# w_down of an encoder layer: fewer pairs in the seven-product form, two pairs in direct form ahead of the tail, other queues and times for some loads and stores

## The chip, the cores and the metric

The kernel runs on one core of a Trainium2 chip. The metric is device time in microseconds (us) of one execution, as the median of several runs. Every profile is one execution under the hardware profiler; its times count from the first instruction's start.

A core has TensorE (matmuls; PE in the profile, PEld its weight loads), VectorE (DVE), ScalarE (ACT), GpSimd (POOL) and SyncE (SP). Each works through its own instructions in order. A transfer is issued by an engine's queue; here nearly all loads are on SP's queue, and those that add to memory on GpSimd's. A queue whose next transfer must wait for something holds up all that stand behind it.

## What is computed

One layer of an encoder on 512 tokens of width 2048, in fp32: a norm, mixed attention, a residual; then a norm, SwiGLU with hidden width 5632, a residual, and a last norm:

```python
    h = rmsnorm(x, ffn_norm_w[l])
    x = x + (jax.nn.silu(h @ w_gate[l]) * (h @ w_up[l])) @ w_down[l]
return rmsnorm(x, final_norm_w)
```

The change concerns the product with w_down (5632 x 2048) and what lies around it. Call g the product of the gated and the up branch; it is 5632 x 512, transposed.

## The kernel before

Every fp32 operand is split into a high part in the rounded type fp32r and a low part (the rest), and each product is three matmuls: high by high, high by low, low by high. ScalarE makes the high part (L196, L1101, L1328: a copy), VectorE the low part by a subtraction (L197, L1106, L1329).

**Gate and up.** `Feed.run` takes w_gate and w_up through 22 blocks of 256 columns. Its matmuls are L1147 to L1149. Two blocks of 256 by 256 by 256 are multiplied with seven products instead of eight; sums of the weights (L1089 to L1091) and of the operands are needed for it. `Feed.finish` multiplies gate and up (L1184, L1188) and writes the result to DRAM, gd[j] for pair j of 128 rows, with a store on SP's queue (L1190).

**w_down, three forms in a row.** The 5632 rows are 22 pairs of 256.

1. *Direct jobs*, `run_job` (L293 to L295): pairs 0 and 1, for each of four columns c of 512 outputs. A job is four halves (128 rows each); a half is 12 matmuls of 512 columns, 3 for each of four token tiles. `st.split(j.first + i + AHEAD)` with AHEAD = 3 splits the weights two halves ahead of the one in work. `g_load` (L1223) and `g_split` (L1231 to L1235) bring g. `evac_down` scales the four banks with ScalarE (L1262), and GpSimd adds them to xd in DRAM (L1264). Between the halves `before_down` calls `dn.make(3)`.
2. *Seven-product form*, class `Down` (L1362 to L1364): pairs 2 to 19 in three chunks of six; in a chunk the four columns, in a column the chunk's six pairs. One pair for one column is a *piece*, 42 matmuls of 256 columns into seven banks. Weights come by L1073 on SP, at most three ahead. `operands`, a generator, loads a pair of g (L1307) and makes its sums and splits (L1313 to L1329); each `make` takes it on to its next `yield`, four to a pair, and `Down.run` calls make(2) each piece. At a column's end ScalarE copies the seven banks out (L1379, L1381), three of them behind the next piece's split (`evac_late`). The first chunk stores them to md in DRAM by SP (L1386), the others add to md by GpSimd (L1384). In the last chunk `combine(c)` follows: seven loads of md (L1401, SP) and four of xd (L1404, GpSimd), two yields later VectorE's sums (L1410, L1411) and scaling (L1424) into x1[c]. It is stepped once a piece by `run_urgent`. The fourth combine, `self.done`, is not on that list; the tail runs it.
3. *Tail*, `finish` (L1515 to L1517): pairs 20 and 21 direct, token tile by token tile. Its weights are loaded by `st.load` (L181) and split by L196 and L197 from piece 2 of the last chunk's last column on, where also g is loaded and split, and the last norm's weights are loaded (`start_tail`). VectorE adds each bank to x1 (`residual`, L1254), ScalarE squares (L394), VectorE multiplies by the last norm's weights (L1524), and `later` scales by the norm's factor (L1501, L1499) and stores (L1502).

**What sets the order.** The code is written out in the order in which each engine has its instructions; there is no scheduler. SBUF is handed out in two pools of slots, 70 of 512 columns (a in the profile) and 16 of 1024 (b), first freed, first used: a transfer waits until the slot's last reader is done.

Of the kernel before, what the change touches and what calls it, by code (L numbers as in the profile page):

```python
# [111 lines left out]
def put(*slots):  # L112
    for s in slots:
        if s.home is not None:
            s.home.free.append(s.i)


def layer(nc, tc, x, attn_norm_w, w_in, rel_table, gw_f, gb_f, gw_b, gb_b, gla_norm_w, w_out,
# [7 lines left out]
    with tc.manual_schedule(), \  # L126
# [136 lines left out]
        def run_job(j):  # L263
# [6 lines left out]
            for i in range(j.n):  # L270
                if j.before:
                    j.before(i)
                st.load()
                st.split(j.first + i + AHEAD)
                _, _, wh, wl = st.halves[j.first + i]
# [836 lines left out]
        class Feed(Blocks):  # L1112
# [66 lines left out]
            def finish(self, u, c_, c):  # L1179
                w, j = self.units[u]  # L1180
                if w is w_gate:
                    tables(SILU)
                    for f in range(2):
                        dve.tensor_tensor(c_.t[:, f], c_.t[:, f], rb[2 + f].t, op=OP.mult)  # L1184
                    act.activation(c_.t, c_.t, AF.Silu)
                    self.gate = c_
                else:
                    dve.tensor_tensor(c_.t, c_.t, self.gate.t, op=OP.mult)  # L1188
                    put(self.gate)
                    sp.dma_start(out=gd[j], in_=c)  # L1190
                    put(c_)
# [47 lines left out]
        def down_start(q):  # L1239
            if q == 0:  # L1240
                g_load(0)
            if q == 1:
                st.until = down_pieces
                st.limit = 3
                st.load()
                g_load(1)
            if q == 2:
                g_split(0)
                st.split(down_first + 2)
            if q == 3:  # L1250
                dn.make(2)

# [33 lines left out]
        class Down(Blocks):  # L1286
# [13 lines left out]
            def operands(self):  # L1300
                a, z = slice(0, 256), slice(256, 512)
                tt = dve.tensor_tensor
                for q in [q for ch in self.chunks for q in ch]:
                    while len(s4.free) < 2:
                        yield
                    r = s4.get(F32, [P, 2, 512])
                    sp.dma_start(out=r.t.rearrange("p f t -> p (f t)"), in_=gd[q])  # L1307
                    yield
                    while len(s2.free) < 9 + 4:
                        yield  # L1310
                    n1, f2 = r.t[:, 1], r.t[:, 0]
# [11 lines left out]
                    for i, (src, hi, lo, hf) in enumerate(todo):  # L1323
# [6 lines left out]
                        if i:  # L1330
                            put((r, t13, t24)[i - 1])
                        if i % 2:
                            yield
# [55 lines left out]
            def evac_late(self):  # L1389
                for e in self.late:  # L1390
                    self.evac(*e)
                if self.late and self.late[0][0] == len(self.chunks) - 1:
                    self.done = self.combine(self.late[0][1])
                    if self.late[0][1] < 3:
                        urgent.append(self.done)
                self.late = []

            def combine(self, c):
# [4 lines left out]
                for t in range(4):  # L1403
                    pool.dma_start(out=x1[c][t].t, in_=xd[4 * c + t])  # L1404
                yield
                yield
                M = [None] + [x_.t for x_ in m]
# [22 lines left out]
            def run(self):  # L1430
                for i, (ch, c, q) in enumerate(self.seq):
# [12 lines left out]
                    if ch == len(self.chunks) - 1 and c == 3:  # L1444
                        n = self.chunks[ch].index(q)
                        if n == 0:
                            g_load(FF // 256 - 2)
                        if n == 1:
                            g_split(FF // 256 - 2)
                            g_load(FF // 256 - 1)  # L1450
                            st.until, st.limit = None, 1
                            start_tail()
                        if n == 2:
                            g_split(FF // 256 - 1)
                        if n >= 2:
                            st.load()
                            st.split(tail_first + 2 * (n - 1))
                self.evac_late()
                st.limit, st.big = 3, tail_first
                drain()  # L1460

# [4 lines left out]
        for c in range(4):  # L1466
            j = job("B", [piece512(w_down, c * 512, k) for k in (0, 2)], list(range(4)),
                    lambda k: gT[k], evac_down(c), before=before_down(c))
            if c == 3:
                j.drop = drop_g  # L1470
        down_pieces = len(st.pieces)
        tail_first = len(st.halves)
        dn = Down([list(range(2, 8)), list(range(8, 14)), list(range(14, 20))])

# [10 lines left out]
        def finish():  # L1485
# [6 lines left out]
            def later(t, ys):  # L1492
# [3 lines left out]
                for c in range(4):  # L1496
                    o = ys[c]
                    if t == 3 and c % 2:
                        act.activation(o.t, o.t, AF.Copy, scale=rstdf[:, t:t + 1])  # L1499
# [5 lines left out]
            def run():  # L1505
                for t in range(4):
                    ys = []
                    for c in range(4):
                        b = ps.get()
                        tok = slice(t * P, (t + 1) * P)  # L1510
                        for k in range(per):
# [5 lines left out]
                            mm(b.t, xl.t[:, tok], wh.t, start=False, stop=k == per - 1)  # L1517
                        if t == 0 and c == 3:
                            for _ in dn.done:
                                pass  # L1520
                        residual(c, t, b)
                        squares(c, t, x1[c], ss2)
                        y = s2.get()
                        dve.tensor_tensor(y.t, x1[c][t].t, wf[c].t, op=OP.mult)  # L1524
                        ys.append(y)
# [4 lines left out]
        run_last = finish()  # L1530
        for n, j in enumerate(jobs):
            run_job(j)
            if n == n_out:
                ff.run()
        dn.run()
        run_last()
# [27 lines left out]
```

## Time and profile before

| | |
|---|---|
| runs (us) | 2270.17, 2269.99, 2267.9 |
| median (us) | 2269.99 |
| the profiled execution (us) | 2269.61 |
| its span, first to last instruction (us) | 2267.8 |
| mean granted TensorE clock in the span | 0.991 |
| HBM read, written (MB) | 246.58, 46.20 |

The profile's page gives the busy time of each engine; other views of the same trace group the instructions by line, list who waited for whom (total us, times, longest), give the instructions in order of time, and give the busy time of each engine in chosen stretches. In a timeline row stand start, length, engine, line, operation, tiles and count; in brackets the idle time before it and what ended it. A busy TensorE includes matmuls that overlap in its pipeline, so that 12 of 0.39 us may start within 2.7 us.

### The profile page before, as it was taken

The numbers are of one execution on the slowest core, as the hardware profiler recorded it, in microseconds if no ns is written. First come the engines' busy times: TensorE is split into PE (matmuls) and PEld (weight loads), VectorE is DVE, ScalarE is ACT, GpSimd is POOL, SyncE is SP. The second block draws the span as 40 slices with busy tenths as digits, with TensorE's granted clock in tenths as the row PEclk, the third lists the DMA queues.
The fourth block names the chain that finished last, engine by engine and source line by source line (L and its number), as shares of the span: only waits on it lengthen the run. The fifth ranks groups of instructions, "written<-read, shape, count | busy, mean of one in ns | idle before, by whom it ended". The sixth has DMA issues, their size and how long they took to land.

```text
span 2267.8 us, 37302 instructions
## 1 busy us (share of the span) xinstructions
PE 2216.3 (98%) x14958; PEld 2046.6 (90%) x14958; DVE 1648.7 (73%) x2749; ACT 1011.5 (45%) x1641; POOL 104.4 (5%) x151
## 2 busy tenths in 40 slices
PE   8999999999999999999999999999999899999977
PEld 7888887888888888999999999999999699999975
DVE  4366665744454456888888888888888777978677
ACT  5244444443454444444334444344443545655343
POOL 0000000000000000000000000000000100122130
PEclk9999999999999999999999999999999999999988
DMA  5524624331324332333333333333334755767884
GB/s 202 156 84 135 194 74 132 103 106 57 101 75 146 124 112 89 117 121 113 127 116 112 122 119 123 112 113 129 114 122 143 204 163 183 212 159 183 252 242 139
DMA packets 211804, 307.78 MB, mean 136 GB/s; under 512 B 15375, under 2 KB 131263, under 8 KB 211632
## 3 DMA queue, kind: packets, MB, share of 16 engines
q1 hardware_dynamic: 195648, 270.90, 37.1%
q0 software_dynamic: 15088, 33.45, 6.9%
q8 instruction: 117, 1.92, 0.3%
q10 hardware_dynamic: 896, 1.06, 0.1%
q14 instruction: 55, 0.45, 0.1%
HBM read 246.58 MB, written 46.20 MB: 129 GB/s over the span
## 4 chain that ended last, share of the span: by engine, by line
PE 79%; issue 12%; DMA 3%; DVE 3%; POOL 1%; ACT 1%; SPq 0%; POOLq 0%; ACTq 0%; DVEq 0%
PE ps L1149 13%; PE ps L1148 13%; PE ps L1147 13%; PE ps L294 5%; PE ps L293 5%; PE ps L295 5%; PE ps L285 5%; PE ps L286 5%; PE ps L287 5%; PE ps L514 1%; POOL md L1384 1%; DMA b<-gd 1%; DMA md<-a 1%; PE ps L841 1%; PE ps L1516 1%
## 5 line engine op out<-in xcount | busy, mean ns | idle before, releaser
L1149 PE MATMUL ps<-a,b 128*128 128x256 f32 x2464 | 697.7, 283 | 2.9 <-DVE b L1106 2.9
L1101 ACT CAST b<-b 128x768 fp32r<-128x768 f32 x496 | 459.8, 942 | 539.4 <-DVE b L1106 381.2
L1147 PE MATMUL ps<-a,b 128*128 128x256 f32 x2464 | 697.4, 283 | 0.0
L1148 PE MATMUL ps<-a,b 128*128 128x256 f32 x2464 | 697.3, 283 | 0.0
L1106 DVE TENSOR_TENSOR b<-b,b 128x768 fp32r<-128x768 f32 x496 | 523.8, 1088 | 137.1 <-PE ps L1148 62.0
L1149 PEld LDWEIGHTS ps<-a,b 128*128 128x128 f32 x2464 | 473.0, 192 | 3.8 <-DVE b L1106 3.8
L1147 PEld LDWEIGHTS ps<-a,b 128*128 128x128 f32 x2464 | 473.1, 192 | 0.0
L1148 PEld LDWEIGHTS ps<-a,b 128*128 128x128 f32 x2464 | 473.1, 192 | 0.0
L1362 PE MATMUL ps<-b,a 128*128 128x256 f32 x1008 | 287.0, 285 | 9.8 <-ACT b L1101 9.8
L1363 PE MATMUL ps<-b,a 128*128 128x256 f32 x1008 | 287.5, 285 | 7.9 <-DVE b L1106 7.9
L1364 PE MATMUL ps<-b,a 128*128 128x256 f32 x1008 | 286.6, 284 | 0.0
L197 DVE TENSOR_TENSOR a<-b,a 128x512 fp32r<-128x512 f32 x280 | 187.2, 687 | 131.6 <-ACT a L196 127.8
L1362 PEld LDWEIGHTS ps<-b,a 128*128 128x128 f32 x1008 | 194.7, 193 | 10.0 <-ACT b L1101 10.0
L1363 PEld LDWEIGHTS ps<-b,a 128*128 128x128 f32 x1008 | 194.7, 193 | 9.5 <-DVE b L1106 9.5
L1364 PEld LDWEIGHTS ps<-b,a 128*128 128x128 f32 x1008 | 194.7, 193 | 0.0
L196 ACT CAST a<-b 128x512 fp32r<-128x512 f32 x280 | 164.5, 617 | 45.1 <-DMA b<-in_w_in_dram 17.9
L1089 DVE TENSOR_TENSOR b<-b 128x512 f32<-128x512 f32 x248 | 169.8, 685 | 19.9 <-DMA b<-in_w_down_dram 15.8
L285 PE MATMUL ps<-a,a 128*128 128x512 f32 x416 | 167.9, 404 | 0.0
L294 PE MATMUL ps<-a,a 128*128 128x512 f32 x400 | 157.8, 394 | 9.0 <-DVE a L197 9.0
L286 PE MATMUL ps<-a,a 128*128 128x512 f32 x416 | 163.0, 392 | 0.0
L287 PE MATMUL ps<-a,a 128*128 128x512 f32 x416 | 163.0, 392 | 0.0
L293 PE MATMUL ps<-a,a 128*128 128x512 f32 x400 | 160.1, 400 | 0.5 <-ACT a L196 0.5
(222 smaller groups left out, 3031.4 us busy)
## 6 DMA issues: line engine op xcount, KB each, us to landing
b<-in_w_gate_dram SPq DMA_DIRECT2D x88, 512.0 KB, 3.4
b<-in_w_up_dram SPq DMA_DIRECT2D x88, 512.0 KB, 3.5
b<-in_w_down_dram SPq DMA_DIRECT2D x88, 512.0 KB, 4.7
b<-in_w_in_dram SPq DMA_DIRECT2D x96, 256.0 KB, 4.5
b<-in_w_in_dram SPq DMA_DIRECT2D x48, 512.0 KB, 3.9
b<-in_w_out_dram SPq DMA_DIRECT2D x32, 512.0 KB, 4.1
md<-a POOLq DMA_DIRECT2D x56, 256.0 KB, 8.7
a<-a SPq DMA_DIRECT2D x96, 128.0 KB, 2.3
```

What stands on the lines that cost most here:

```text
L285: mm(o, wh.t[:, c], xh.t, start=first, stop=False)
L286: mm(o, wh.t[:, c], xl.t, start=False, stop=False)
L287: mm(o, wl.t[:, c], xh.t, start=False, stop=last)
L293: mm(o, xh.t[:, c], wh.t[:, w], start=first, stop=False)
L1101: act.copy(hi.t, src)
L1106: dve.tensor_tensor(lo.t, src, hi.f, op=OP.subtract)
L1147: mm(o, wh, xh, start=head, stop=False, skip_group_check=True)
L1148: mm(o, wh, xl, start=False, stop=False, skip_group_check=True)
L1149: mm(o, wl, xh, start=False, stop=end, skip_group_check=True)
L1362: mm(o, xh[:, t], wh, start=first and h == 0, stop=False, skip_group_check=True)
L1363: mm(o, xh[:, t], wl, start=False, stop=False, skip_group_check=True)
L1364: mm(o, xl[:, t], wh, start=False, stop=last, skip_group_check=True)
```

## The change

- The chunks of the seven-product form are 6, 5 and 5 pairs (2 to 7, 8 to 12, 13 to 17). Pairs 18 and 19 become four more direct jobs between the last chunk and the tail; VectorE adds their banks to x1 (`residual`) instead of ScalarE and GpSimd to xd. They split further ahead: two halves for each half in work, so that the tail's weights are split when the last of them ends.
- The store of gd[j] is on GpSimd's queue.
- `operands` keeps up to two loads of g ahead and has three yields a pair; the call ahead of the first direct job is make(1).
- `combine` waits three steps behind its loads (five for the last column) instead of two, and all four combines are on the urgent list; `drain` runs what is left after the new jobs, ahead of the tail.
- In the last column of the chunks g and the first weights of the new jobs are loaded, in place of the tail's; `start_tail` is called after the chunks.
- For the first three token tiles of the tail one operation (L1528 of the new kernel) multiplies by the norm's factor and by its weights, in place of two.

```diff
-                st.split(j.first + i + AHEAD)
+                st.split(j.first + i + AHEAD + (4 * j.tail + i if hasattr(j, "tail") else 0))
...
-                    sp.dma_start(out=gd[j], in_=c)
+                    pool.dma_start(out=gd[j], in_=c)
...
-                dn.make(2)
+                dn.make(1)
...
-                for q in [q for ch in self.chunks for q in ch]:
-                    while len(s4.free) < 2:
+                qs = deque(q for ch in self.chunks for q in ch)
+                raws = deque()
+
+                def load():
+                    if qs and len(s4.free) > 1 and len(raws) < 2:
+                        r = s4.get(F32, [P, 2, 512])
+                        sp.dma_start(out=r.t.rearrange("p f t -> p (f t)"), in_=gd[qs[0]])
+                        raws.append((qs.popleft(), r))
+
+                load()
+                load()
+                yield
+                while raws or qs:
+                    load()
+                    if not raws or len(s2.free) < 9 + 4:
                         yield
-                    r = s4.get(F32, [P, 2, 512])
-                    sp.dma_start(out=r.t.rearrange("p f t -> p (f t)"), in_=gd[q])
-                    yield
-                    while len(s2.free) < 9 + 4:
-                        yield
+                        continue
+                    q, r = raws.popleft()
...
+                        if i == 1:
+                            load()
...
-                    self.done = self.combine(self.late[0][1])
-                    if self.late[0][1] < 3:
-                        urgent.append(self.done)
+                    urgent.append(self.combine(self.late[0][1]))
...
-                yield
-                yield
+                for _ in range(3 if c < 3 else 5):
+                    yield
...
                         if n == 0:
-                            g_load(FF // 256 - 2)
-                        if n == 1:
-                            g_split(FF // 256 - 2)
-                            g_load(FF // 256 - 1)
+                            g_load(LAST // 2 - 2)
+                        if n == 2:
+                            g_split(LAST // 2 - 2)
+                            g_load(LAST // 2 - 1)
                             st.until, st.limit = None, 1
-                            start_tail()
-                        if n == 2:
-                            g_split(FF // 256 - 1)
-                        if n >= 2:
                             st.load()
-                            st.split(tail_first + 2 * (n - 1))
+                        if n > 2:
+                            st.split(later_first + n - 2)
                 self.evac_late()
                 st.limit, st.big = 3, tail_first
-                drain()
+
+        def evac_later(c):
+            def f(banks):
+                for t in range(4):
+                    residual(c, t, banks[t])
+            return f
+
+        def before_later(c):
+            def f(i):
+                j = LAST // 2 - 2 + (c + 1)
+                if c and i == 0:
+                    g_load(j)
+                if i == (2 if c else 0) and c < 3:
+                    g_split(j)
+            return f
...
+        n_down = len(jobs)
+        later_first = len(st.halves)
+        for c in range(4):
+            j = job("B", [piece512(w_down, c * 512, k) for k in (LAST - 4, LAST - 2)], list(range(LAST - 4, LAST)),
+                    lambda k: gT[k], evac_later(c), before=before_later(c), rate=1.0)
+            j.tail = c
+            if c == 3:
+                j.drop = drop_g
         tail_first = len(st.halves)
-        dn = Down([list(range(2, 8)), list(range(8, 14)), list(range(14, 20))])
+        dn = Down([list(range(2, 8)), list(range(8, 13)), list(range(13, 18))])
...
-                    if t == 3 and c % 2:
+                    if t < 3:
+                        dve.scalar_tensor_tensor(o.t, x1[c][t].t, rstdf[:, t:t + 1], wf[c].t,
+                                                 op0=OP.mult, op1=OP.mult)
+                    elif c % 2:
...
-                        if t == 0 and c == 3:
-                            for _ in dn.done:
-                                pass
...
-                        dve.tensor_tensor(y.t, x1[c][t].t, wf[c].t, op=OP.mult)
+                        if t == 3:
+                            dve.tensor_tensor(y.t, x1[c][t].t, wf[c].t, op=OP.mult)
...
         for n, j in enumerate(jobs):
+            if n == n_down:
+                dn.run()
+                start_tail()
             run_job(j)
             if n == n_out:
                 ff.run()
-        dn.run()
+        drain()
         run_last()
```

The loads and sums of the changed kernel have new line numbers: its seven-product matmuls are L1374 to L1376, its operand sums L1323 to L1339.

## The prediction

> **What bounds the kernel now.** I read the page first, then the stages, then who waits inside them. From the page:
>
> ```profile
> PE 2216.3 (98%) x14958; PEld 2046.6 (90%) x14958; DVE 1648.7 (73%) x2749; ACT 1011.5 (45%) x1641; POOL 104.4 (5%) x151
> ```
>
> TensorE is busy for 98% of the span, but that is a mean. The windows by stage (us; PE, PEld, DVE, ACT, POOL busy, then granted clock, DMA share, GB/s) show where it is not:
>
> ```profile
> 900.00:1750.00 850.00, 850.00 (x7086) 850.00 (x7085) 744.40 (x1122) 347.00 (x401) 0.00 (x0) 1.00 0.37 119
> 1819.00:1940.00 121.00, 121.00 (x1009) 120.92 (x1009) 95.64 (x145) 65.83 (x91) 3.54 (x4) 1.00 0.54 175
> 1761.00:1819.00 58.00, 48.48 (x198) 38.53 (x197) 44.29 (x89) 31.89 (x61) 10.64 (x12) 0.91 0.72 198
> 2061.00:2091.00 30.00, 29.36 (x243) 28.95 (x242) 29.38 (x46) 16.73 (x24) 5.65 (x8) 1.00 0.68 166
> 2091.00:2124.00 33.00, 29.36 (x232) 29.16 (x232) 19.91 (x29) 11.71 (x17) 7.25 (x10) 0.95 0.84 225
> 2124.00:2154.00 30.00, 30.00 (x252) 30.00 (x251) 23.85 (x36) 13.76 (x19) 8.40 (x11) 1.00 0.97 263
> 2154.00:2205.00 51.00, 37.82 (x294) 36.91 (x294) 36.52 (x55) 24.23 (x37) 13.64 (x19) 0.87 0.80 247
> 2205.00:2258.00 53.00, 47.79 (x195) 38.11 (x194) 45.45 (x88) 17.51 (x47) 5.34 (x8) 0.94 0.52 150
> ```
>
> In the gate/up stage TensorE is never idle. In the seven-product form it starts 1009 matmuls in 121.00 us: 0.120 us each, **5.04 us a piece** of 42. The timeline of TensorE gives the stage borders and the price of a direct matmul:
>
> ```profile
> 1761.61 0.40 PE L293 MATMUL ps<-a,a 128*128 128x512 f32 x1
> ...
> 1815.88 0.39 PE L293 MATMUL ps<-a,a 128*128 128x512 f32 x1
> ...
> 1818.60 0.39 PE L293 MATMUL ps<-a,a 128*128 128x512 f32 x1
> ...
> 1819.28 0.28 PE L1362 MATMUL ps<-b,a 128*128 128x256 f32 x1
> ...
> 2205.17 0.40 PE L1515 MATMUL ps<-a,a 128*128 128x512 f32 x1
> ...
> 2257.85 0.39 PE L1517 MATMUL ps<-b,a 128*128 128x512 f32 x1
> ```
>
> The second and third rows are 12 matmuls, one half, apart: 2.72 us, 0.227 us each. So four direct jobs (192 matmuls, 16 halves) cost 43.5 us. The losses follow. The first direct jobs take 1761.6 to 1819.3, 57.7 us: **14.2 lost**. Two chunks of 24 pieces would end at 1819.3 + 241.9 = 2061.2, the third at 2182.2; it ends at 2205.2: **23.0 lost**. The tail, another 192 matmuls, takes 52.9: **9.4 lost**. After its last matmul 9.7 us remain to the end of the span (2267.8). That is 46.6 us in all. TensorE's waits in the program name the reasons:
>
> ```profile
> PE ps L1362 <- ACT b L1101: 9.8, 1, 9.8
> PE ps L294 <- DVE a L197: 9.0, 3, 6.6
> PE ps L1363 <- DVE b L1106: 7.9, 7, 3.6
> ...
> PE ps L1515 <- ACT b L196: 4.8, 2, 2.7
> ```
>
> Behind them stand SP's queue (waits, then its timeline) and, for the longest, ScalarE's timeline:
>
> ```profile
> SPq L1401 <- DMA md<-a: 38.2, 21, 7.7
> ...
> SPq L1190 <- DVE b L1188: 17.3, 1, 17.3
> ```
>
> ```profile
> 2093.65 15.62 SPq L1401 DMA_DIRECT2D a<-md  x7
> 2109.38 14.05 SPq L1073 DMA_DIRECT2D b<-in_w_down_dram  x5
> ```
>
> ```profile
> 2172.33 7.07 SPq L1401 DMA_DIRECT2D a<-md  x7
> 2181.43 19.77 SPq L181 DMA_DIRECT2D b<-in_w_down_dram  x8
> ```
>
> ```profile
> 2189.17 1.14 ACT L196 CAST a<-b 128x512 fp32r<-128x512 f32 x2 [6.64 <-DMA b<-in_w_down_dram]
> 2190.22 1.77 ACT L1101 CAST b<-b 128x768 fp32r<-128x768 f32 x2
> ```
>
> Three times SP stands still with loads behind it: 17.3 us at the last store of g, 15.6 at the first combine's loads, 7.1 at the third's. The last holds back the tail's weights until 2181.4; ScalarE, in order, waits for them ahead of the last pieces' L1101, and TensorE waits for that 9.8 us.
>
> **The change part by part.** *Matmuls.* Eight pieces of 5.04 (40.3 us) go, four direct jobs (43.5) come: **+3.2**. Without any wait the new kernel would need 1761.6 + 43.5 + 64 x 5.04 + 43.5 + 43.5 + 9.7 = **2224.4**. Now the waits that stay or come.
>
> *First direct jobs.* The store of g leaves SP for GpSimd, so SP's 17.3 us go; operand loads run two ahead. VectorE's waits for g go (8.3 us in this stage); the second fence is its timeline:
>
> ```profile
> DVE a L1313 <- DMA b<-gd: 8.3, 3, 5.1
> ```
>
> ```profile
> 1773.48 0.69 DVE L197 TENSOR_TENSOR a<-b,a 128x512 fp32r<-128x512 f32 x1
> 1774.09 1.22 DVE L1188 TENSOR_TENSOR b<-b,b 128x1024 f32<-128x1024 f32 x1
> ...
> 1793.04 0.42 DVE L1313 TENSOR_TENSOR a<-b 128x256 f32<-128x256 f32 x1
> ...
> 1797.25 0.42 DVE L1313 TENSOR_TENSOR a<-b 128x256 f32<-128x256 f32 x1
> ```
>
> But VectorE is next. One pair's operands with one half's L197 take it 1797.25 - 1793.04 = 4.21 us; TensorE eats a half in 2.72. The program order of the new kernel puts a whole pair's operands ahead of each L197, for halves 2 to 8; before, some calls of make went on a load alone. Half 4's L197 started at 1773.48; now two L1329 (1.2 us) that came behind it stand before it, and, as an estimate, 0.8 us of waiting for ScalarE, since g_split(1) now comes ahead of the first pair; it ends at 1773.48 + 0.69 + 2.0 = 1776.2. TensorE wants it at 1761.6 + 4 x 2.72 = 1772.5. Then L1188 (1.1) and four times 4.21: half 8 is ready at 1794.1, and eight halves end at 1815.9. **10.8 lost** instead of 14.2. Bounds: 0, if VectorE kept up; 18, if nothing were won and one pair more (3.6), which the new order has ahead of half 7, came on top of 14.2. I take the sum of rows.
>
> Here the clock matters: the stage of 33 us above, with a wait of 3.6, had a granted clock of 0.95, so about 3.3 us at half speed, 1.65 lost. My wait before half 4 is 3.7 us, but TensorE waits for VectorE in the next halves anyway, so I add nothing. The Trainium skill, TensorE: Matmul & The Clock Gate, "What's actually happening", says that an idle window of about 3.4 us drops the clock to half; the rows agree. By that rule a drop falling late in the stage would add 1.7, mine has 0.
>
> *Stores of g on GpSimd.* No row has such a store. Its nearest are the same bytes from SP, and 256 KB from GpSimd:
>
> ```profile
> gd<-b SPq DMA_DIRECT2D x22, 512.0 KB, 2.7
> ...
> xd<-a POOLq DMA_DIRECT2D x32, 256.0 KB, 3.3
> ```
>
> ```profile
> L1384 POOL DMA_DIRECT2D md<-a x56 | 49.5, 1205 | 319.4 <-ACT a L1381 309.4 <-ACT a L1379 9.7 <-ACT a L1328 0.2
> ```
>
> Twenty-two issues of 1.2 us lie in a stage where GpSimd does nothing (0.00) and TensorE is full: 0. If each stopped VectorE for its 1.2 us, that is 27 us of the 106 that VectorE has idle in 850: still 0. Nothing waits for these stores soon but g's last pairs.
>
> *Chunks.* Each piece costs VectorE 3.6 us:
>
> ```profile
> 1825.74 2.08 DVE L1106 TENSOR_TENSOR b<-b,b 128x768 fp32r<-128x768 f32 x2
> ...
> 1829.62 2.10 DVE L1106 TENSOR_TENSOR b<-b,b 128x768 fp32r<-128x768 f32 x2 [0.27 <-PE ps L1364]
> ```
>
> The pair that starts at 1829.62 is piece 4's, done at 1831.7, and TensorE starts that piece at 1819.3 + 4 x 5.04 = 1839.4: a lead of 7.7. The new make needs three calls a pair, not four, so six pairs (4.21 less L197's 0.61: 3.6 each) fall on nine pieces instead of twelve: 54.0 of VectorE against 45.4 of TensorE, 0.9 beyond the lead; I take **1.5**. The first combine still starts in the first piece of column 1, right behind the accumulations that it reads, so SP's 15.6 us stay and with them 3.6 + 1.65: **5.3**. The second now starts three pieces into column 2, long after column 1's sums are written; SP issues seven loads but waits for none: 0 to 5, I take **1.5**. The third and fourth fall into the new jobs, so nothing holds up the first weights behind the chunks, which are asked for three pieces ahead: the 9.8 goes. Chunks: **8.3** lost (was 23.0).
>
> *The new jobs.* VectorE gets 16 more L1254 and loses ScalarE's help:
>
> ```profile
> L1254 DVE SCALAR_TENSOR_TENSOR a<-ps,small,a 128x512 f32<-128x512 f32 x16 | 11.9, 746 | 3.9 <-PE ps L1517 3.9
> ```
>
> Those 11.9, thirty L197 at 0.61 (1773.48 to 1774.09: 18), the third combine (eleven operations of this kind and size: 7) and two g_splits (2.4) are 39 us beside 43.5 of TensorE. Two halves are split per step, so the lead grows; **1** lost, from 0 to 8. *Tail.* All its weights are split by then: its waits for L196 go, **1** lost of 9.4. The fourth combine (7 us of VectorE) has eight banks, 8 x 2.72 = 22 us of TensorE, to hide in; for three of four token tiles one L1528 replaces two operations, off the path.
>
> Sum: 2224.4 + 10.8 + 8.3 + 1 + 1 = **2245.5**, 22 less than the span of 2267.8. The profiled execution took 2269.61, 1.8 beside its span, and the median of the runs shown is 2269.99: **2247.5**, 22 (1.0%) under it.
>
> **Rivals.** *A. The DMA engines become the bound* (slower). From 2061 to 2205 they were busy 30 x 0.68 + 33 x 0.84 + 30 x 0.97 + 51 x 0.80 = 118 us.
>
> ```profile
> q1 hardware_dynamic: 195648, 270.90, 37.1%
> ```
>
> 37.1% of 2267.8 us for 270.90 MB is 3.1 us per MB. Up to the tail's start the change takes four weight loads of 0.52 MB out and puts eight in, adds two of g and the fourth combine's eleven of 0.26: (6 x 0.52 + 2.9) x 3.1 = 18.7. That is 137 us in 64 + 80 = 144 (20 pieces and four jobs). At a share of 0.95 it fits, and the tail's weights may slip behind. If the engines reach only the 0.80 of the last stretch and nothing slips, it takes 171, 27 over: 2245.5 + 27 + 1.8 = 2274, slower. It turns the result below a share of 0.82. For it: the stretches at 0.84 and 0.80 are those that stall. Against: 30.00 of 30.00 at a share of 0.97. The Trainium skill, DMA: Bandwidth & Descriptors, "Issuing engines are not separate DMA queues", stands on its side: all issuers share the same 16 engines, and another issuer saves only issuing time. The 17.3 us above are a wait in the issuer, of which that rule says nothing.
>
> *B. It does not do what it says.* The wait ahead of the chunks' end comes back at the new jobs (9.8, its clock and what follows it: 15 of the 23.0) and the tail keeps 7: 2269, no change. For it: loads of g still stand in SP's queue there. Against: no combine does.
>
> *C. VectorE keeps up in the first jobs.* Their 10.8 vanish: 2237. For it: 8.3 us of waiting for g go. Against: 4.21 against 2.72.
>
> **How the numbers follow.** Forecast 0.62 (2240 to 2260 with its own bounds), A 0.14, B 0.13, C 0.11. The range, 2235 to 2268, takes in forecast and C and reaches to B. A measurement of this kernel tells 0.2%, 4.5 us, from no change. Faster: forecast, C and half of B, 0.79; same: the rest of B, 0.07; slower: A, 0.14.
>
> **What would show it.** First L1374 near 1816, with VectorE, not a load of g, ahead of the late halves. SP's wait at the store of g gone; its long stop at loads of md once, not thrice. No wait of TensorE of 9 us at the end of the chunks; the tail within 45 us. Wrong if L1374 starts after 1820, if the DMA share of the last chunk is under 0.85 while TensorE waits for loads of w_down, or if the new jobs take over 50 us.

## The result and the profile after

| kernel | median (us) | lowest to highest | runs |
|---|---|---|---|
| before | 2270.08 | 2267.9 to 2270.24 | 4 |
| after | 2248.94 | 2248.44 to 2250.48 | 4 |

The ratio is 0.991, with a 95% interval of 0.9893 to 0.9927: 21 us faster; the forecast was 2247.5, 22 us faster. The profiled execution took 2248.97 us and its span is 2247.2. The busy line of its page, to set beside that of before:

```profile
PE 2213.8 (99%) x14814; PEld 2038.0 (91%) x14814; DVE 1633.1 (73%) x2717; ACT 1001.7 (45%) x1637; POOL 116.3 (5%) x173
```

It says as little as before; the stages say more. The timeline of TensorE in the changed kernel gives their borders (start, length, line; the first row starts the first direct jobs, then come the chunks, the new jobs, the tail, and the last matmul):

```profile
1763.06 0.40 PE L293 MATMUL ps<-a,a 128*128 128x512 f32 x1
...
1817.30 0.28 PE L1374 MATMUL ps<-b,a 128*128 128x256 f32 x1
...
2150.51 0.40 PE L293 MATMUL ps<-a,a 128*128 128x512 f32 x1
...
2194.05 0.39 PE L1547 MATMUL ps<-b,a 128*128 128x512 f32 x1
...
2237.35 0.39 PE L1549 MATMUL ps<-a,a 128*128 128x512 f32 x1
```

The first direct jobs take 54.2 us for 43.5 of matmuls: 10.7 lost. The chunks take 333.2 for 64 x 5.04 = 322.6: 10.6 lost. The new jobs take 43.5 and the tail 43.5: nothing lost. TensorE's waits in the changed kernel from the first direct job on are down to three groups (total us, times, longest); the 9.8 ahead of the chunks' end and those at the tail's weights are no longer in the list:

```profile
PE ps L1375 <- DVE b L1106: 6.9, 8, 3.2
PE ps L294 <- DVE a L197: 4.2, 4, 1.1
PE ps L293 <- ACT a L196: 2.5, 2, 1.5
```

The windows by stage (us; PE, PEld, DVE, ACT, POOL busy, granted clock, DMA share, GB/s):

```profile
1763.00:1817.00 54.00, 47.14 (x193) 36.63 (x193) 42.60 (x86) 30.36 (x57) 11.17 (x13) 0.97 0.82 215
1938.00:1964.00 26.00, 22.93 (x183) 21.91 (x182) 25.62 (x44) 14.53 (x24) 0.00 (x0) 1.00 0.64 218
2085.00:2105.00 20.00, 16.76 (x127) 16.56 (x126) 13.69 (x21) 7.95 (x12) 6.42 (x9) 0.91 0.75 220
2105.00:2150.00 45.00, 45.00 (x377) 45.00 (x376) 38.00 (x56) 22.50 (x32) 10.97 (x15) 1.00 1.02 287
2150.00:2194.00 44.00, 44.00 (x198) 36.53 (x197) 35.05 (x57) 21.20 (x37) 10.00 (x16) 1.00 1.01 330
2194.00:2238.00 44.00, 43.74 (x193) 35.87 (x192) 36.65 (x71) 13.22 (x39) 0.00 (x0) 1.00 0.25 85
```

Three places lose most of what is still lost: the first direct jobs, the stretch from 1938 to 1964 with VectorE busy for 25.62 of 26 us (it makes the operands of several pairs in a row there; such a stretch is called a burst below), and the one around 2090. At the last stands the one stop that SP has left; its timeline shows the loads of md of the four combines:

```profile
2070.80 14.78 SPq L1411 DMA_DIRECT2D a<-md  x7
...
2115.04 3.80 SPq L1411 DMA_DIRECT2D a<-md  x7
...
2143.71 5.43 SPq L1411 DMA_DIRECT2D a<-md  x7
...
2187.53 3.40 SPq L1411 DMA_DIRECT2D a<-md  x7
```

The first still takes 14.8 us (15.6 before); the others are short. SP's wait at the store of g is gone, since the store (L1190) is on GpSimd's queue.

### The profile page after: what moved, and what is told of

Same layout as the page of the kernel before. It is cut to its first block, busy times and chain, and to the rows that moved or that the text cites. A ratio compares the mean times of both kernels' runs of the same rounds, so it can differ in the third digit from the quotient of the medians.

```text
span 2247.2 us, 37030 instructions
## 1 busy us (share of the span) xinstructions
PE 2213.8 (99%) x14814; PEld 2038.0 (91%) x14814; DVE 1633.1 (73%) x2717; ACT 1001.7 (45%) x1637; POOL 116.3 (5%) x173
## 4 chain that ended last, share of the span: by engine, by line
PE 92%; DVE 5%; ACT 1%; DMA 1%; issue 1%; SPq 0%; ACTq 0%; DVEq 0%
PE ps L1149 13%; PE ps L1148 13%; PE ps L1147 13%; PE ps L294 6%; PE ps L293 6%; PE ps L295 6%; PE ps L285 5%; PE ps L286 5%; PE ps L287 5%; PE ps L1375 4%; PE ps L1376 4%; PE ps L1374 4%; PE ps L514 1%; DVE b L1106 1%; DVE a L1339 1%; PE ps L841 1%
## 5 line engine op out<-in xcount | busy, mean ns | idle before, releaser
L1101 ACT CAST b<-b 128x768 fp32r<-128x768 f32 x480 | 445.5, 943 | 550.8 <-DVE b L1106 318.8
L1106 DVE TENSOR_TENSOR b<-b,b 128x768 fp32r<-128x768 f32 x480 | 509.3, 1088 | 137.7 <-PE ps L1148 62.2
L197 DVE TENSOR_TENSOR a<-b,a 128x512 fp32r<-128x512 f32 x292 | 195.0, 686 | 135.8 <-ACT a L196 128.6
L1375 PE MATMUL ps<-b,a 128*128 128x256 f32 x896 | 255.2, 285 | 6.9 <-DVE b L1106 6.9
L1376 PE MATMUL ps<-b,a 128*128 128x256 f32 x896 | 254.3, 284 | 0.0
L1374 PE MATMUL ps<-b,a 128*128 128x256 f32 x896 | 254.2, 284 | 0.0
L196 ACT CAST a<-b 128x512 fp32r<-128x512 f32 x292 | 171.4, 617 | 53.1 <-DMA b<-in_w_in_dram 18.1
L293 PE MATMUL ps<-a,a 128*128 128x512 f32 x464 | 184.5, 398 | 2.5 <-ACT a L196 2.5
L294 PE MATMUL ps<-a,a 128*128 128x512 f32 x464 | 182.1, 392 | 4.4 <-DVE a L197 4.2
L295 PE MATMUL ps<-a,a 128*128 128x512 f32 x464 | 181.6, 391 | 0.0
L1375 PEld LDWEIGHTS ps<-b,a 128*128 128x128 f32 x896 | 172.6, 193 | 8.7 <-DVE b L1106 8.7
L1089 DVE TENSOR_TENSOR b<-b 128x512 f32<-128x512 f32 x240 | 164.0, 683 | 22.4 <-DMA b<-in_w_down_dram 18.5
L1374 PEld LDWEIGHTS ps<-b,a 128*128 128x128 f32 x896 | 172.7, 193 | 0.0
L1376 PEld LDWEIGHTS ps<-b,a 128*128 128x128 f32 x896 | 172.7, 193 | 0.0
L285 PE MATMUL ps<-a,a 128*128 128x512 f32 x416 | 168.3, 405 | 0.0
L286 PE MATMUL ps<-a,a 128*128 128x512 f32 x416 | 163.4, 393 | 0.0
```

What stands on the lines that cost most here:

```text
L285: mm(o, wh.t[:, c], xh.t, start=first, stop=False)
L293: mm(o, xh.t[:, c], wh.t[:, w], start=first, stop=False)
L294: mm(o, xh.t[:, c], wl.t[:, w], start=False, stop=False)
L295: mm(o, xl.t[:, c], wh.t[:, w], start=False, stop=last)
L1101: act.copy(hi.t, src)
L1106: dve.tensor_tensor(lo.t, src, hi.f, op=OP.subtract)
```

## The experiments

My theory after this: the direct pairs take away the losses at the chunks' end and in the tail; the other edits win only in the first direct jobs, where VectorE is the limit, and the rewritten `operands` costs the burst of 1938 to 1964. Rivals: the queue edits carry the gain; the first direct jobs are limited by loads, not VectorE; the rest is a matter of DMA engines. The table has all runs; "lost" is a stage's length on TensorE less its matmuls (43.5 us for 192 direct ones, 0.120 for each of the seven-product form); it is that of the one profiled execution, which can be some us from the median (best3: 2233.33, the longest of its four). The ratios are to runs of the kernel before on the same chip; its medians there were 2268.7 to 2270.8, so differences of medians below are good to a microsecond or two.

| kernel | median (us) | ratio to before, 95% | lost: first direct jobs | chunks | new jobs | tail |
|---|---|---|---|---|---|---|
| before | 2270.08 | | 14.2 | 23.0 | | 9.4 |
| after | 2248.94 | 0.9893 to 0.9927 | 10.7 | 10.6 | 0.0 | 0.0 |
| direct_only | 2247.58 | 0.9878 to 0.9908 | 14.3 | 7.3 | 0.0 | 0.0 |
| no_direct | 2270.85 | 0.9993 to 1.0011 | 10.8 | 24.6 | | 12.1 |
| store_back | 2253.82 | 0.9905 to 0.9938 | 16.5 | 11.5 | 0.0 | 0.0 |
| before_store | 2260.45 | 0.9939 to 0.9969 | 6.6 | 21.7 | | 9.3 |
| direct_store | 2239.09 | 0.9848 to 0.9881 | 6.9 | 4.0 | 0.0 | 0.0 |
| yield4 | 2243.88 | 0.9877 to 0.9909 | 13.9 | 3.9 | 0.0 | 0.0 |
| make2 | 2244.83 | 0.9880 to 0.9908 | 8.0 | 10.6 | 0.0 | 0.0 |
| comb0_late | 2252.61 | 0.9915 to 0.9944 | 10.8 | 12.2 | 0.0 | 0.0 |
| best | 2234.71 | 0.9837 to 0.9865 | 0.0 | 7.8 | 0.0 | 0.0 |
| best3 | 2230.98 | 0.9814 to 0.9843 | 0.0 | 6.5 | 0.0 | 0.0 |
| comb_pool | 2228.98 | 0.9805 to 0.9834 | 0.1 | 0.7 | 1.5 | 0.1 |
| md_twice | 2319.03 | 1.0196 to 1.0226 | 10.7 | 51.4 | 19.7 | 7.4 |

### The change taken apart: direct_only, no_direct

direct_only is the changed kernel with these parts as before:

```diff
-                    pool.dma_start(out=gd[j], in_=c)
+                    sp.dma_start(out=gd[j], in_=c)
...
-                dn.make(1)
+                dn.make(2)
...
-                qs = deque(q for ch in self.chunks for q in ch)
...
+                for q in [q for ch in self.chunks for q in ch]:
...
-                for _ in range(3 if c < 3 else 5):
+                for _ in range(2):
```

no_direct is the kernel before with the same parts (and the one operation for two at the end of the tail) as in the changed one.

> The two direct pairs and their place alone (chunks of 6, 5 and 5, the new jobs, the new order of the tail); the store of g is on SP's queue, operand loads one ahead with four yields a pair, and the combine two yields behind its loads, all as in the kernel before. My theory (the direct pairs take away the losses at the chunks' end and in the tail, the other edits only the 3.5 us of the first direct jobs): the new jobs and the tail take 43.5 us each as in the changed kernel, the first direct jobs lose about 14 as before, and the loss of 3.9 us at the bursts of operands (1938 to 1963 in the changed kernel) is gone or under 1, since a pair's operands are spread over four calls: 2250, give or take 4. Rival: without the loads further ahead SP's stop at the store of g and the combine's sums two pieces behind their loads hold up the last chunk and the new jobs too: over 2257.

> The other half of the change: chunks of six pairs and the tail as before, with the store of g on GpSimd's queue, the operand loads two ahead, the combine three yields behind its loads, and the one operation for two in the tail's end. My theory: the first direct jobs lose 10.7 instead of 14.2, the chunks' end still waits some 10 us for the tail's weights behind the loads of md, the tail still loses 9.4: 2266, from 2263 to 2270. Rival (the queue edits alone carry the gain): under 2256.

Measured: 2247.58 and 2270.85. The direct pairs alone give what the whole change gives, the rest alone gives nothing (2263 to 2270 had been expected of it). Which part of direct_only gives it, the shorter chunks, the splits further ahead or the place of the last combines, was not taken apart. direct_only loses 14.3 in the first direct jobs as before, nothing in the new jobs and the tail, and TensorE is busy for all of 26 us where the changed kernel has its burst. Its waits on TensorE, and that stretch:

```profile
PE ps L294 <- DVE a L197: 9.9, 5, 6.6
PE ps L1363 <- DVE b L1106: 5.3, 2, 4.6
```

```profile
1938.00:1964.00 26.00, 26.00 (x219) 26.00 (x218) 25.59 (x44) 18.08 (x29) 0.75 (x2) 1.00 0.68 234
```

Against after, the front is 3.6 worse and the chunks are 3.3 better. So the edits beside the pairs take in one place what they give in another. no_direct won its 3.4 in the first direct jobs and gave them back: 1.6 in the chunks, 2.7 in the tail. The rival of the queue edits falls.

### The store of g alone: before_store, store_back

```diff
-                    sp.dma_start(out=gd[j], in_=c)
+                    pool.dma_start(out=gd[j], in_=c)
```

before_store is this line in the kernel before; store_back is its reverse in the changed kernel.

> The kernel before with only the store of g moved to GpSimd's queue. My theory: SP's stop of 17.3 us is gone, and with it VectorE's 8.3 us of waiting for loads of g in the first direct jobs; they lose 8 to 11 instead of 14.2, the rest stays: 2264, from 2262 to 2268. Rival (VectorE was the limit there anyway, the loads only moved its idle time): within 1 us of the kernel before.

> The changed kernel with the store of g on SP's queue again. My theory: SP stands still at the last store for about 17 us again, the first loads of g of the operands come that much later, VectorE waits for them and the first direct jobs lose 14 or more instead of 10.7: 2 to 8 us over the changed kernel, all of it in the first direct jobs. Rival (the loads two ahead cover it): within 1 us of the changed kernel.

before_store took 9.6 to 10.3 us off (2260.45, against 2270.08 and, on its own chip, 2270.76): more than expected, because the first direct jobs lose only 6.6, not the 8 to 11 that I had worked out. Of it 7.6 are won there and 1.3 in the chunks. TensorE's waits in these jobs fall from 9.5 to 4.5 us, and its granted clock in them rises from 0.91 to 1.00 (0.09 of 57.7 us are 5.2): a good part of the 7.6 goes with the clock, of which the theory had nothing. The rival, that VectorE was the limit anyway, falls for the kernel before. store_back is 4.9 slower than the changed kernel, and loses 16.5 in the first direct jobs against 10.7, as expected. Loads two ahead do not cover SP's stop:

```profile
SPq L1190 <- DVE a L1323: 17.7, 1, 17.7
```

So the store is worth 10 us in the old operands, and all of no_direct, which contains it, is worth nothing. Something in the rest of the change takes it back.

### What takes it back: direct_store

The changed kernel with `operands` and the call make(2) as before; store, pairs and combine stay as changed.

```diff
-                dn.make(1)
+                dn.make(2)
...
-                qs = deque(q for ch in self.chunks for q in ch)
...
+                for q in [q for ch in self.chunks for q in ch]:
```

> The changed kernel with operands and the call of make ahead of the first direct jobs as in the kernel before (loads one ahead, four yields a pair); the direct pairs, the store on GpSimd's queue and the combine's three yields stay. Known by now: the direct pairs alone came to 2247.6, the store alone took 10 us off the kernel before (its first direct jobs lost 6.7), all edits without the direct pairs took nothing. My theory: the store and the direct pairs add, and the rewritten operands, which put a pair's work into three steps, give the store's gain back; without it the first direct jobs lose 6.7 instead of 10.8 and the bursts go: 2240, from 2238 to 2243. Rival (the gains overlap, the two stages share one limit): 2246 or more.

Measured 2239.09, 9.9 less than the changed kernel: the rewritten `operands`, with its call of make, costs 10 us. 3.8 of it lie in the first direct jobs, 6.6 in the chunks (the bursts, and a drop of the clock that is told of below). TensorE's waits:

```profile
PE ps L294 <- DVE a L197: 4.9, 5, 1.5
PE ps L1363 <- DVE b L1106: 3.5, 2, 3.3
```

Only the first combine's wait is left in the chunks. The gains of the store and of the pairs add to within 2 us (10.3 and 23.2 alone, 31.5 together, each against before on its own chip); the rival of a shared limit falls.

### How much of a pair between two halves: yield4, make2

```diff
+                    yield
                     q, r = raws.popleft()
```

```diff
-                dn.make(3)
+                dn.make(2)
```

> The changed kernel with a fourth yield a pair in operands, between the load and the first sums, so that a call of make does less of a pair. My theory: what the changed kernel loses in the bursts at 1938 to 1963 (3.9 us) is VectorE making six pairs in nine pieces; with four calls to a pair they fall on twelve pieces, 54 us of VectorE against 60 of TensorE, and the loss goes to under 0.5. In the first direct jobs fewer operations stand ahead of each L197, so their loss falls from 10.7 by some us too: 4 to 7 us faster than the changed kernel. Rival (the stalls there come from something else, ScalarE's copies or the store of md): the loss at 1938 to 1963 stays, within 1.5 us.

> The changed kernel with make(2) instead of make(3) between the halves of the first direct jobs. My theory (VectorE is the limit there: 4.21 us a half against TensorE's 2.72): with two thirds of a pair's work to a half VectorE needs about 3.0 a half, and the loss falls from 10.7 to about 4; the pairs not made there fall into the first chunk, where VectorE has 1.4 us of idle time a piece: 5 to 7 us faster than the changed kernel. Rival: the missing pairs come due in the first chunk, whose pieces then wait for operands: same or slower, with waits of TensorE for L1328 or L1339 in the first six pieces.

yield4: 2243.88, 5.1 less than after. The bursts went (their pieces take 5.04 us each again, and the chunks lose 3.9 instead of 10.6), so the first half of its theory holds. The second half fails: the first direct jobs lose 13.9, more than before the edit. TensorE's waits there are 7.9 us, against 6.7 in the changed kernel, and its granted clock is 0.91 against 0.97: most of the difference goes with the clock. make2: 2244.83, 4.1 less; the loss there falls to 8.0, not to 4, and nothing comes due in the first chunk, so its rival falls too. What I had left out shows in ScalarE's waits of the changed kernel, of make2 and of yield4, in these jobs:

```profile
ACT a L196 <- DMA xd<-a: 2.4, 1, 2.4
```

```profile
ACT a L196 <- DMA xd<-a: 5.7, 1, 5.7
```

```profile
ACT a L196 <- DMA xd<-a: 8.4, 2, 4.4
```

The split of the weights waits for slots that hold bank copies on their way to xd. In the changed kernel this wait costs nothing (TensorE never waits behind 1795.6 in these jobs); in make2 TensorE waits 2.7 us for the split behind it, its longest wait there. So VectorE is not the only limit. Why this wait is 8.4 in yield4, and 2.4 in the changed kernel as in best3 below, was not settled.

### The first combine later: comb0_late, best

```diff
             def combine(self, c):
+                for _ in range(2 if c == 0 else 0):
+                    yield
                 m = [s2.get(F32, [P, 2, 256]) for _ in range(7)]
```

best has this, yield4's line and make2's.

> The changed kernel with the first combine's loads asked for two pieces later. My theory: SP stands still for 14.8 us there because the adds to md that the loads wait for have only just been issued; two pieces (10 us) later most of that wait is gone, weights come in time, and the wait of 3.4 us at 2090 and the half clock behind it (3.4 us, 1.7 lost) go: 4 to 5 us faster than the changed kernel. Rival (the weights are late because the DMA engines are busy, not because SP stands still): within 1.5 us.

> The three together: four yields a pair, make(2) in the first direct jobs, the first combine two pieces later. If they add, each as its theory says, 10 to 15 us faster than the changed kernel, 2234 to 2239. Rival: with fewer steps a call and two calls a half the first pairs' operands come too late for the first chunk, and it is slower than the changed kernel in the first six pieces.

comb0_late: 2252.61, 3.7 slower than after: 1.6 in the chunks, 2.1 behind the last matmul (best, with the same edit, does not have these 2.1). The theory was right on the place and wrong on the sum. SP's first stop shrank from 14.78 to 3.89 and the wait at 2090 went. But the combines are stepped one at a time, so the second came later too; its SP and ScalarE timelines:

```profile
2081.42 3.89 SPq L1413 DMA_DIRECT2D a<-md  x7
...
2120.98 4.77 SPq L1413 DMA_DIRECT2D a<-md  x7
...
2128.92 2.68 SPq L1223 DMA_DIRECT2D b<-gd  x2
```

```profile
2142.75 0.63 ACT L1231 ACTIVATE a<-b 128x512 fp32r<-128x512 f32 x1 [12.92 <-DMA b<-gd]
...
2143.80 1.77 ACT L1101 CAST b<-b 128x768 fp32r<-128x768 f32 x2
```

The loads of g for the new jobs now stand right behind the second combine's seven; ScalarE waits 12.9 us for them ahead of a piece's L1101, and TensorE waits 3.2 at the chunks' end, with a stretch at a low clock behind it (0.66 from 2145 to 2150). This is the wait of rival B of the prediction, with loads of g in place of weights. But SP's order is only part of it: SP issued the first of these loads 3.1 us later than in the changed kernel (2128.92 for 2125.86), and then it took 13.7 us to land, against 11.8; the combine's seven took 9.8 to 16.2 us, against 5.4 to 5.9. The DMA share was 1.05 to 1.10 from 2125 to 2140. So the DMA engines of rival A have a part in it; how much, no run separates. best shows the same wait (3.8), and gains because yield4 and make2 together leave nothing lost in the first direct jobs: 2234.71, within the 2234 to 2239 expected.

### Without the later combine, and another queue for it: best3, comb_pool

best3 is yield4's line and make2's alone. comb_pool adds:

```diff
-                    sp.dma_start(out=m[n].t.rearrange("p s c -> p (s c)"), in_=md[7 * c + n])
+                    pool.dma_start(out=m[n].t.rearrange("p s c -> p (s c)"), in_=md[7 * c + n])
```

> Four yields a pair and make(2) between the halves of the first direct jobs, with the first combine where the changed kernel has it. My theory: the first direct jobs lose nothing as with all three edits, the chunks lose the 3.9 that they lose with four yields alone (the first combine's wait, no wait at the chunks' end): 2230, up to 2232 if the wait is long enough for the half clock. Rival: the wait at the chunks' end that came with the later combine comes from the faster front and stays: 2235.

> As the last, with the seven loads of md of each combine on GpSimd's queue, where the adds to md stand that they wait for; their place in the order of the program stays. My theory: SP no longer stands still, the weights behind the first combine come in time and the wait of 3.3 us there goes: 3 to 5 us faster than the last. Rival (the weights and g are late because the DMA engines are full): the wait moves to a later place, as it did when the first combine came two pieces later, and the time is within 1.5 us of the last or above it.

best3: 2230.98, as expected; the wait at the chunks' end is gone, so it came with the later combine, not with the faster front. comb_pool: the wait behind the first combine is gone, the chunks lose 0.7 instead of 6.5, and TensorE is busy throughout at a DMA share of 1.07 and 1.02 (2060 to 2080). All of TensorE's waits from the first direct job on:

```profile
PE ps L1548 <- DVE a L1254: 1.3, 1, 1.3
PE ps L1376 <- DVE b L1106: 0.2, 1, 0.2
```

So it was SP standing still, not full DMA engines, that made the weights late there. The gain in time is less sure than the mechanism: the medians are 2.0 us apart, not 3 to 5, and the runs (2229.84 to 2233.33, and 2228.68 to 2230.17) overlap; best3's profile shows its longest run. 1.5 us come back as TensorE's wait for VectorE at the end of the new jobs. This is the fastest of these kernels, 20 us under the changed one.

### More load on the DMA engines: md_twice

```diff
-                    sp.dma_start(out=m[n].t.rearrange("p s c -> p (s c)"), in_=md[7 * c + n])
+                    for _ in range(2):
+                        sp.dma_start(out=m[n].t.rearrange("p s c -> p (s c)"), in_=md[7 * c + n])
```

> The changed kernel with every load of md for the combines issued twice into the same buffers, 7.3 MB more and, at 3.1 us a MB, some 23 us more of all DMA engines between 2070 and 2194, where the changed kernel has their share near 1.0 and waits of TensorE at one place only. My theory (these stages fit with some slack, since the tail's loads can slip into the tail, where the share is 0.25): over 5 and under 15 us slower, with new waits at the chunks' end as those of the later first combine. Rival (the engines are at their limit): 20 us or more slower. Second rival (a share of 1.0 does not mean that they are full): under 3.

Measured 2319.03: 70 us slower than after, far outside what the theory gave. But it did not test what it was to test. A second load into the same buffer waits until the first has landed, and SP stands still meanwhile; its timeline and waits:

```profile
2070.59 32.79 SPq L1412 DMA_DIRECT2D a<-md  x14
2131.91 34.56 SPq L1412 DMA_DIRECT2D a<-md  x14
2183.91 41.06 SPq L1412 DMA_DIRECT2D a<-md  x14
2249.90 23.75 SPq L1412 DMA_DIRECT2D a<-md  x14
```

```profile
SPq L1412 <- DMA a<-md: 106.4, 28, 9.0
```

```profile
2130.00:2180.00 50.00, 29.42 (x224) 29.22 (x224) 22.37 (x32) 14.39 (x20) 6.23 (x7) 0.76 0.68 197
```

The four stops are 132 us instead of 27, and the DMA share falls to 0.68 while TensorE waits: the engines are not the limit of md_twice, the queue is. What room the engines have in the changed kernel stays open; it shows what 105 us of standing still in SP cost here, about 70.

## Why the prediction was right, and where it was wrong

The total was 1.4 us off, the span 1.7 (2247.2 for 2245.5). By the prediction's steps:

- **First direct jobs**, 10.8: 10.7. VectorE's rows show the walk as it was laid out, a whole pair of operands ahead of each L197, 4.21 us from one to the next:

```profile
1782.85 0.42 DVE L1323 TENSOR_TENSOR a<-b 128x256 f32<-128x256 f32 x1
...
1786.45 0.68 DVE L197 TENSOR_TENSOR a<-b,a 128x512 fp32r<-128x512 f32 x1
1787.06 0.41 DVE L1323 TENSOR_TENSOR a<-b 128x256 f32<-128x256 f32 x1
...
1794.87 1.28 DVE L197 TENSOR_TENSOR a<-b,a 128x512 fp32r<-128x512 f32 x2
```

```profile
1795.61 0.50 PE L294 MATMUL ps<-a,a 128*128 128x512 f32 x1 [1.02 <-DVE a L197]
```

  The first L197 of the row at 1794.87 is half 8's. It ends at 1795.55, 1.4 behind the forecast's 1794.1, in a stage that started 1.5 late; eight halves of 2.72 from there end at 1817.3, as measured. So this is no luck. The clock is as forecast too: it was 0.97 in the stage, and that cost nothing, since TensorE waits for VectorE again behind its drop (the second row). direct_store and best3, with less of a pair ahead of a half, lose 6.9 and 0.0. What I had not seen is that this is a cost of the change: the store alone would have left 6.6.
- **Stores of g on GpSimd**, 0 in the gate/up stage: no wait of TensorE there was added by them, and an issue took 0.533 us, not 1.2:

```profile
L1190 POOL DMA_DIRECT2D gd<-b x22 | 11.7, 533 | 896.6 <-DVE b L1188 896.6
```

- **Chunks**, 8.3: 10.6. Here the step failed that sizes the operands' bursts at 1.5. By the lengths of the pieces they cost 4.4 from 1938 to 1968 and 1.1 from 2034 to 2045 (0.2 more are lost in the chunks' second piece). The work was right: VectorE's L1106 started 5.7 to 6.2 us apart there, against 5.04 of TensorE. The lead was wrong. The wait that names its pair is this (VectorE, then TensorE):

```profile
1938.58 2.09 DVE L1106 TENSOR_TENSOR b<-b,b 128x768 fp32r<-128x768 f32 x2
...
1944.24 2.09 DVE L1106 TENSOR_TENSOR b<-b,b 128x768 fp32r<-128x768 f32 x2
...
1950.17 2.09 DVE L1106 TENSOR_TENSOR b<-b,b 128x768 fp32r<-128x768 f32 x2
...
1956.37 2.08 DVE L1106 TENSOR_TENSOR b<-b,b 128x768 fp32r<-128x768 f32 x2
```

```profile
1938.49 0.28 PE L1374 MATMUL ps<-b,a 128*128 128x256 f32 x1
1939.58 0.39 PE L1375 MATMUL ps<-b,a 128*128 128x256 f32 x1 [0.81 <-DVE b L1106]
```

  Counted back seven pieces, VectorE's row and TensorE's first matmul of the same piece are:

```profile
1898.33 0.96 DVE L1106 TENSOR_TENSOR b<-b,b 128x768 fp32r<-128x768 f32 x1 [1.16 <-PE ps L1375]
```

```profile
1903.21 0.28 PE L1374 MATMUL ps<-b,a 128*128 128x256 f32 x1
```

  VectorE is done with the first of the piece's two operations at 1899.3, 3.9 ahead, and had to wait 1.16 for TensorE to free the slot: here the slots, not VectorE, set the lead. The prediction gave the pair at 1829.62 to a piece one too late and so read 7.7; one piece earlier it is 2.7 to the end of both its operations, 3.8 to that of the first. With 3.9 its own sum is 54.0 - 45.4 - 3.9 = 4.7, against the 4.4. In no_direct, with six pairs a chunk and the same `operands`, the bursts are there too; in direct_only, direct_store and yield4 they are not.
- **The first combine**, 5.3: a wait of 3.2 and 20 us at a clock of 0.91 (1.8), 5.0. comb_pool shows the cause, SP's stop. **The second**, 1.5: 0. **New jobs** and **tail**, 1 each: 0.
- The **front** of the program started the first direct job at 1763.1 instead of 1761.6, which is 1.5 of the 1.7. The kernels here, which share that part, have it between 1761.5 and 1763.1.
- **Rival A** did not come: the share was 1.02 and 1.01 from 2105 to 2194, over the 0.82 from which it decides, with TensorE busy throughout. comb0_late comes nearest to it. **Rival B**'s wait did not come either, but two pieces of delay bring it. **Rival C** is not what the change does, but what best3 does.

So the forecast was right with its mechanism, but that the total is only 1.4 off is in part luck: the bursts cost 4.0 more than forecast, and the two combines, the new jobs and the tail together 3.8 less. It did not say that the 21 us are 31 from the direct pairs and the store (direct_store) less 10 from the new `operands`.

## What to carry to other kernels

Where an engine fills gaps with work cut into steps, look at how much of it stands ahead of each urgent operation: here the first direct jobs lost 10.7 us with a whole pair's operands ahead of each half, and nothing with half a pair. It is not all that counts: with three quarters of a pair they lost 6.9 in direct_store and 13.9 in yield4. In an in-order queue one transfer that must wait holds up every load behind it (17.3 us of SP here, and 10 us of the kernel); move it to a queue with nothing urgent behind it. And take a change of several edits apart in both directions before believing its total: here one edit paid for another's loss.

## What the runs showed of the hardware

The clock's price of a wait was not one number. yield4 and best3 have the same row of TensorE's waits behind the first combine; the fences are that row in yield4 and its two windows, then those of best3:

```profile
PE ps L1376 <- DVE b L1106: 3.4, 2, 3.1
```

```profile
2075.00:2090.00 15.00, 11.88 (x100) 11.67 (x99) 6.05 (x10) 1.88 (x2) 0.00 (x0) 1.00 1.05 352
2090.00:2105.00 15.00, 15.00 (x126) 15.00 (x127) 14.76 (x22) 8.75 (x13) 8.39 (x11) 1.00 0.71 138
```

```profile
2065.00:2080.00 15.00, 11.88 (x87) 11.67 (x86) 7.47 (x11) 3.09 (x4) 0.00 (x0) 0.87 0.84 313
2080.00:2095.00 15.00, 15.00 (x116) 15.00 (x116) 14.76 (x23) 8.15 (x13) 8.38 (x11) 0.91 0.92 166
```

One kept a clock of 1.00; the other had 0.87 and 0.91, 15 x 0.13 + 15 x 0.09 = 3.3 us, of which 2.6 show in the loss of the chunks (6.5 against 3.9). In the changed kernel a wait of 3.2 cost 1.8, in direct_store one of 3.3 nothing. The Trainium skill, TensorE: Matmul & The Clock Gate, "What's actually happening", says that the chip watches a free-running window of about 3.4 us and halves TensorE's clock after an idle one. Here the clock fell behind single waits of 3.1 and 3.2 and not behind others of 3.1 and 3.3, so the length of the wait alone does not decide; what does, no run shows. It differs between runs of one kernel too: best3's four runs had mean clocks of 0.997, 0.998, 0.999 and 0.999 and took 2233.33, 2231.73, 2230.23 and 2229.84 us. So some 2 us of difference between kernels with such waits may be chance.

Nor is a single long wait needed. In the first direct jobs of the changed kernel no wait was over 1.5 us, yet the granted clock was 0.50 from 1784 to 1786; four waits of 1.0 to 1.5 us stood in the 10 us before.

The DMA share read 1.02 and 1.01 over 89 us in which TensorE, fed by those transfers, was never idle: a full share is no proof of a bound. In comb0_late a share of 1.05 to 1.10 went with loads of 13.7 us and a wait: the share alone does not tell the two apart.
